# Hybrid diffusion backbone: modulation sums on VectorE in halves, gates kept as rows

## The chip, the cores and the metric

One core of a Trainium2 chip runs the whole program in one launch. The metric is device time in microseconds, the median of three executions; a profile of one more execution gives the trace.

## The reference, cut to what matters

Two layers act on 256 latent tokens and 256 context tokens of width 1024, all in fp32. What the change touches is the adaptive modulation: each layer has one matrix `w_ada` of 1024 x 6144, and two condition vectors are multiplied with it, one for the latent tokens, one for the context.

```python
for layer in range(2):
    need_ctx = layer < 1
    ada_lat = silu(c) @ w_ada[layer] + b_ada[layer]          # 6144 numbers
    ada_ctx = silu(c_ctx) @ w_ada[layer] + b_ada[layer]
    sh1, sc1, g1, sh2, sc2, g2 = split(ada_lat, 6)           # and the same for ada_ctx
    u = modulate(rmsnorm(h, gains[0]), sh1, sc1)             # x * (1 + scale) + shift
    p = u @ w_in[layer]                                      # feeds three parallel mixers
    m = merge(hyena(p), rglru(p), hgrn2(p)) @ w_out[layer]
    h = h + g1 * rmsnorm(m, gains[1])
    f = square(relu(modulate(rmsnorm(h, gains[2]), sh2, sc2) @ w_mlp1[layer])) @ w_mlp2[layer]
    h = h + g2 * rmsnorm(f, gains[3])
```

The second layer needs the context only where the mixers scan through it, so `g1`, `sh2`, `sc2`, `g2` are needed there for the latent tokens alone. The Hyena mixer also needs, once per layer, an implicit filter (a small network with two sines, then a Fourier transform); the kernel calls this `filters(l)`.

## The kernel before

**Products.** Every large matrix is split into a high part (rounded by ScalarE, `wh`) and a low part (the rest, by VectorE, `wl`), and every product is three matmuls. A weight of 1 MB comes by DMA into one of two raw buffers (`ra`), is split at priority 400, and serves 48 matmuls of 512 columns in layer 0. The split parts have four buffers each.

**Modulation.** The 6144 columns of `w_ada` are taken as three thirds of 2048. Third 0 holds shift 1 and scale 1, third 1 holds gate 1 and shift 2, third 2 holds scale 2 and gate 2. In the names below a pair such as (0,1) is layer and third.
- Third (0,0) is needed at once and is made by `ada_first` on TensorE, in quarters.
- Third (0,1) is made by `ada_steps` on TensorE: eight steps, each a load of 1 MB into a raw buffer and four matmuls with a stationary operand of 32 columns, placed on the four column groups of the array, so that they run side by side.
- (0,2), (1,0), (1,1), (1,2) are made by `ada_sums` on VectorE: a *plan* loads four tiles of 128 x 512 (256 KB each) into the four buffers `AM`, and VectorE multiplies each with one column of the condition (`cst`) and adds it to a sum. With both conditions wanted, a plan takes eight such instructions, otherwise four. The sums still lie across 128 partitions; one group of four matmuls with a stationary operand that has ones in one column (`sel`) adds the partitions up.
- `ada_out` copies the four rows out of PSUM, turns all 2048 values into columns by four transposes, adds the bias to them, and, for thirds 1 and 2, also makes gate rows (times the gain, through DRAM, later broadcast by `gate_rows`).

`AM` serves the HGRN2 mixer too, which relies on zeros in it; `ada_sums` ends with four zeroing instructions on GpSimd.

**Order.** The program is written in one order; a scheduler at build time lists it per engine, taking by a model of the durations the ready instruction with the best priority (written order, moved up inside `high_priority`). So work that is ready early can stand ahead of where it is written, if its buffers are free. In passages marked `InOrder.fixed` the listed order is kept as written. Background work comes from the queue `bg`: a list of generators, of which `bg.step()` runs the first one up to its next `yield`, and `bg.drain()` runs all to the end. In layer 0 there is one `bg.step()`:
- for each weight of the input projection that is used (lines 1300 to 1316), and in the merge of the three branches for each weight of the gates and of the branch projections (2 after the first branch's gates, then 4 + 2, then 4 + 2);
- for each of 16 weights of the first MLP product (line 1636), then for each of 8 and 6 weights of the second one (`pump`, line 1648).

`bg.drain()` stands ahead of the output projection (line 1528), and in `start_next` (line 1651), which is called at the layer boundary inside `junction`: the first of four token tiles has its residual, then `norm()` calls `start_next`, then come the norm of tile 0, tile 1 likewise, and a passage in fixed order with transposes, modulation and the first products of layer 1. `groups(filters(1), (9, 4, 4, 9))` cuts the 26 pieces of the second layer's filters into four steps.

```python
        def norm():
            if not holder: holder.append(start_next())   # bg.drain(); lnexp(); Norm(...)
...
        for i in range(2):
            products(i, 0)
            products(i, 1)
            residual(first[i], p[i], G, i)
            n = norm()
            n.tile(i)
```

**Tables.** `era(name)` loads an activation table and orders all later activations that need a table (`fn`) behind it, and itself behind all earlier ones. `filters` asks for the set with Sin; `lnexp()` for that with Ln and Exp, which each residual and each norm uses.

`tmp()` takes one of 14 buffers of 128 x 512, `blk()` one of 49; a PSUM bank comes from `psm()` (`pm`, large products) or `psx()` (`px`, the rest).

Of the kernel before, what the change touches and what calls it, by code (L numbers as in the profile page):

```python
# [96 lines left out]
def prepare(inp):  # L97
# [11 lines left out]
    for w in range(2):  # L109
        for n in range(2):  # L110
            c = (w + 1) * 2048 + (2 * w + n) * 512
            for l in range(2):
                for r in range(2):
                    o = 32 * (2 * n + r) + w if (l, w) == (0, 1) else 32 * (2 * w + n) + r
                    rows[l, w, o] = g["norm_gains"][l, 1 + 2 * w, n * 512:n * 512 + 512]
                    bias[l, w, o] = g["b_ada"][l, c:c + 512]
# [46 lines left out]
def _body(ctx, tc, I, out, cfg):  # L163
# [153 lines left out]
    AM = []  # L317
# [8 lines left out]
    sel = kt([128, 2, 32])  # L326
    pool.memset(sel, 0.0)
    for r in range(2):
        pool.memset(sel[:, r, r:r + 1], 1.0)
# [42 lines left out]
    def ada_steps(l, s):  # L372
        acc = psx('a')
        for k in range(8):
            raw = raw_tile()
            dma(raw, I["w_ada"][l, k * 128:k * 128 + 128, s * 2048:s * 2048 + 2048])
            with tc.high_priority(cfg["AP"]):
                for j in range(4):
                    mm(acc[32 * j:32 * j + 32, :], cst[:, k, :], raw[:, j * 512:j * 512 + 512], k == 0, k == 7,
                       tile_position=(0, 32 * j))  # L380
            yield
        ada_out(l, s, acc, "(j r)")
        yield

    def ada_out(l, s, acc, order):
# [3 lines left out]
        pt = psx('a')  # L389
        for b in range(4):  # L390
            pe.transpose(pt[:, b * 128:b * 128 + 128], rows[:, b * 128:b * 128 + 128], ident)
        cols = kt([128, 2, 2, 8], name="ac")
        if order == "(j r)":
            pv = pt.rearrange("p (b m n r) -> p r m n b", b=4, m=2, n=2)
        else:
            pv = pt.rearrange("p (b n r m) -> p r m n b", b=4, n=2, r=2)[:, :, :2]
        for r in range(2):
            for m in range(2):
                add(cols[:, r, m].rearrange("p (n b) -> p n b", b=4), pv[:, r, m],
                    col(l, "ba", 16 * s + 8 * m, 8).rearrange("p (n b) -> p n b", b=4))  # L400
        ada_cols[l, s] = cols
        if s > 0:
            w, j0 = s - 1, 2 * (s - 1)
# [6 lines left out]
            for n in range(2):  # L410
                if order == "(j r)":
                    dma(st[:, n, :], gr[32 * (j0 + n):32 * (j0 + n) + 2, :])
                    continue
# [1420 lines left out]
```

## Time and profile before

| | |
|---|---|
| median of 3 runs | 1487.9 us (1484.55 to 1488.62) |
| the profiled execution | 1488.52 us, of which the span of the trace is 1486.7 us |
| busy: TensorE, VectorE, ScalarE, GpSimd | 1456.6, 1072.7, 745.4, 25.2 us |
| VectorE sums of `ada_sums` | 168 multiply-adds (117.3 us) and 24 multiplications (10.3 us) |
| matmuls of `ada_steps` | 64 records of two passes each over 32 matmuls (8.3 us) |
| mean granted TensorE clock | 0.995 of full speed |

Times in the trace are microseconds from the span's start. Busy matmuls include waiting inside the array's pipeline, so the start of the next matmul tells more than a matmul's own duration. In a group of instructions, `px<-t,k` names what is written (PSUM tile `px`) and what is read (the moving operand `t`, the stationary operand `k`); buffer numbers are left out. All helpers stand in one line of the source (L220), so the tiles' names tell the work apart: `k` stands for any tile that is kept, `AM` and `cst` among them.

### The profile page before, as it was taken

How to read it: one execution, taken by the hardware profiler on the slowest of the kernel's cores; microseconds unless marked ns; L12 is line 12 of the kernel's file. 1: busy time of each engine (PE TensorE's matmuls, PEld its weight loads, DVE VectorE, ACT ScalarE, POOL GpSimd, SP SyncE). 2: the span in 40 equal slices, each digit the busy share in tenths (PEclk: the TensorE clock that was granted, in tenths of full speed). 3: DMA queues.
4: the chain of work that ended last, by engine and by line, in shares of the span. 5: the costliest groups of instructions: out<-in, count | busy, mean ns of one | idle time of the engine just before them, and what ended most of it. 6: DMA issues, size and time to landing. Idle time of an engine off the chain costs nothing.

```text
span 1486.7 us, 21716 instructions
## 1 busy us (share of the span) xinstructions
PE 1456.6 (98%) x8326; PEld 1224.5 (82%) x8326; DVE 1072.7 (72%) x1853; ACT 745.4 (50%) x1188; POOL 25.2 (2%) x245
## 2 busy tenths in 40 slices
PE   8999999999999999999999999999999999999998
PEld 4766878888888888888887877798889999899986
DVE  6776397978996277755757985776799886866544
ACT  6476565642232425543331223568877745565433
POOL 1000000000000000000000000000000000000000
PEclk9999999999999999999999999999999999999999
DMA  9644321232562242545745534132325335445553
GB/s 316 233 182 160 127 86 58 73 112 86 177 242 91 99 140 88 176 157 189 269 147 208 201 130 141 58 143 85 114 88 178 147 138 204 156 171 186 198 196 113
DMA packets 56999, 225.38 MB, mean 152 GB/s; under 512 B 6448, under 2 KB 8112, under 8 KB 37312
## 3 DMA queue, kind: packets, MB, share of 16 engines
q1 hardware_dynamic: 55168, 220.86, 42.3%
q10 hardware_dynamic: 1728, 3.15, 0.6%
q8 instruction: 65, 1.06, 0.3%
q14 instruction: 38, 0.31, 0.1%
HBM read 220.80 MB, written 3.18 MB: 151 GB/s over the span
## 4 chain that ended last, share of the span: by engine, by line
PE 82%; DVE 9%; ACT 5%; issue 2%; DMA 1%; SPq 0%; DVEq 0%; POOL 0%; ACTq 0%; POOLq 0%
PE pm L220 73%; PE px L220 9%; DVE b L220 4%; DVE t L220 2%; DVE wl L220 2%; ACT b L220 2%; ACT t L220 2%; ACT wh L220 1%; DVE s L220 1%; ACT L220 1%; DMA h<-in_x_dram 1%; DMA k<-in_w_ada_dram 0%; DMA ra<-in_w_ada_dram 0%; DVE h L220 0%; ACT s L220 0%
## 5 line engine op out<-in xcount | busy, mean ns | idle before, releaser
L220 PE MATMUL pm<-b,wh 128*128 128x512 f32 (+1 forms) x3264 | 822.0, 342 | 1.7 <-DVE b L220 1.7
L220 PEld LDWEIGHTS pm<-b,wh 128*128 128x128 f32 x3264 | 564.0, 190 | 76.2 <-issue 3.5
L220 PE MATMUL pm<-b,wl 128*128 128x512 f32 (+1 forms) x1632 | 556.8, 341 | 0.0
L220 ACT ACTIVATE wh<-ra 128x1024 fp32r<-128x1024 f32 x278 | 293.5, 1060 | 498.2 <-PE pm L220 485.3
L220 DVE TENSOR_TENSOR wl<-ra,wh 128x1024 fp32r<-128x1024 f32 x278 | 338.4, 1222 | 243.1 <-ACT wh L220 235.3
L220 PEld LDWEIGHTS pm<-b,wl 128*128 128x128 f32 x1632 | 310.3, 190 | 34.7 <-issue 1.3
L220 PE MATMUL pm<-wh,b 128*128 128x512 f32 x976 | 304.3, 392 | 1.1 <-DVE b L220 1.1
L220 PEld LDWEIGHTS pm<-wh,b 128*128 128x128 f32 x976 | 182.4, 188 | 46.3 <-issue 3.6
L220 PE MATMUL pm<-wl,b 128*128 128x512 f32 x488 | 190.7, 391 | 0.0
L220 DVE TENSOR_TENSOR b<-b,b 128x512 fp32r<-128x512 f32 (+2 forms) x179 | 120.5, 681 | 30.4 <-PE pm L220 14.7
L220 DVE SCALAR_TENSOR_TENSOR t<-k,k,t 128x512 f32<-128x512 f32 x168 | 117.3, 747 | 15.6 <-DMA k<-in_w_ada_dram 15.6
L220 PEld LDWEIGHTS pm<-wl,b 128*128 128x128 f32 x488 | 91.6, 188 | 20.5 <-issue 1.6
L220 PE MATMUL pm<-b,b 128*128 128x256 f32 (+1 forms) x456 | 77.3, 324 | 2.3 <-DVE b L220 2.3
L220 ACT ACTIVATE t<-t 128x512 f32<-128x512 f32 (+3 forms) x124 | 60.8, 526 | 30.7 <-DVE t L220 29.6
L220 PEld LDWEIGHTS pm<-b,b 128*128 128x128 f32 x456 | 66.7, 190 | 10.1 <-DVE b L220 3.6
L220 ACT ACTIVATE t<-pm 128x512 f32<-128x512 f32 (+1 forms) x74 | 42.4, 574 | 35.8 <-PE pm L220 33.3
L220 ACT ACTIVATE b<-pm 128x512 f32<-128x512 f32 x88 | 50.5, 583 | 18.9 <-PE pm L220 10.9
L220 PE MATMUL px<-b,b 128*128 128x128 f32 (+1 forms) x280 | 55.3, 344 | 2.1 <-ACT b L220 1.3
L220 ACT ACTIVATE b<-b 128x512 f32<-128x512 f32 (+1 forms) x80 | 48.7, 627 | 10.7 <-DVE b L220 9.6
L220 ACT ACTIVATE b<-b,k 128x512 f32<-128x512 f32 x64 | 45.7, 739 | 8.6 <-DVE b L220 8.3
L220 PEld LDWEIGHTS px<-b,b 128*128 128x128 f32 x280 | 38.4, 190 | 12.6 <-issue 6.0
L220 ACT ACTIVATE t<-px 128x384 f32<-128x384 f32 (+3 forms) x50 | 21.9, 438 | 46.8 <-PE px L220 46.6
(114 smaller groups left out, 1060.3 us busy)
## 6 DMA issues: line engine op xcount, KB each, us to landing
ra<-in_w_mlp_dram SPq DMA_DIRECT2D x63, 1024.0 KB, 4.9
ra<-in_w_in_dram SPq DMA_DIRECT2D x58, 1024.0 KB, 4.9
k<-in_w_ada_dram SPq DMA_DIRECT2D x128, 256.0 KB, 3.8
ra<-in_w_proj_dram SPq DMA_DIRECT2D x12, 1024.0 KB, 4.8
b<-in_w_ada_first_dram SPq DMA_DIRECT2D x32, 256.0 KB, 5.3
ra<-in_w_ada_dram SPq DMA_DIRECT2D x8, 1024.0 KB, 5.8
ra<-in_w_out_dram SPq DMA_DIRECT2D x8, 1024.0 KB, 5.2
ra<-in_w_i_dram SPq DMA_DIRECT2D x4, 1024.0 KB, 4.7
```

Of the source, the lines that this page charges most:

```text
L220: r = f(*a, **k)
```

## The change

- `ada_steps` is gone: (0,1) is summed by `ada_sums`.
- A job of `ada_sums` is now (layer, third, half), where a half of 1024 columns with both conditions takes four plans of eight instructions, and a third with one condition (half `None`) eight plans of four. Two lists take the place of the old ones. In the merge of layer 0: (0,1) first and second half, (0,2) first half, without zeroing. After the output projection: (0,2) second half, (1,0) in halves, (1,1), (1,2), with zeroing. So it is 12 plans where there were 8, then 28 where there were 24.
- Each half is reduced and handed to `ada_out` by itself. A half that is a gate gets no transposes and no columns. A third with one condition gets columns for one.
- `modulation(1, 1)` fills in one stream; the layouts of `gate_rows` and `sel` follow.

```diff
--- before.py
+++ after.py
@@ -110,8 +110,8 @@
         for n in range(2):
             c = (w + 1) * 2048 + (2 * w + n) * 512
             for l in range(2):
-                for r in range(2):
-                    o = 32 * (2 * n + r) + w if (l, w) == (0, 1) else 32 * (2 * w + n) + r
+                for r in range(2 - l):
+                    o = 32 * (2 * n + r) if l == 0 else 32 * (2 * w + n)
                     rows[l, w, o] = g["norm_gains"][l, 1 + 2 * w, n * 512:n * 512 + 512]
                     bias[l, w, o] = g["b_ada"][l, c:c + 512]
     a["gate_rows"] = np.stack([rows, bias], axis=3)
@@ -323,10 +323,9 @@
 
     cst = kt([128, 8, 32])
     pool.memset(cst, 0.0)
-    sel = kt([128, 2, 32])
+    sel = kt([128, 32])
     pool.memset(sel, 0.0)
-    for r in range(2):
-        pool.memset(sel[:, r, r:r + 1], 1.0)
+    pool.memset(sel[:, 0:1], 1.0)
     csg = kt([128, 8, 2])
     sigmoid()
     fn(csg, cc, AF.Sigmoid)
@@ -369,38 +368,28 @@
         mul(a0[:, ::-1, ks], part[:, :, 0], col(0, "gain0", 2 * qr, 2)[:, None, :].to_broadcast([128, 2, 2]))
         yield
 
-    def ada_steps(l, s):
-        acc = psx('a')
-        for k in range(8):
-            raw = raw_tile()
-            dma(raw, I["w_ada"][l, k * 128:k * 128 + 128, s * 2048:s * 2048 + 2048])
-            with tc.high_priority(cfg["AP"]):
-                for j in range(4):
-                    mm(acc[32 * j:32 * j + 32, :], cst[:, k, :], raw[:, j * 512:j * 512 + 512], k == 0, k == 7,
-                       tile_position=(0, 32 * j))
-            yield
-        ada_out(l, s, acc, "(j r)")
-        yield
-
-    def ada_out(l, s, acc, order):
+    def ada_out(l, s, acc, half):
 
         rows = tmp()
         dve.tensor_copy(rows, acc)
-        pt = psx('a')
-        for b in range(4):
-            pe.transpose(pt[:, b * 128:b * 128 + 128], rows[:, b * 128:b * 128 + 128], ident)
-        cols = kt([128, 2, 2, 8], name="ac")
-        if order == "(j r)":
-            pv = pt.rearrange("p (b m n r) -> p r m n b", b=4, m=2, n=2)
-        else:
-            pv = pt.rearrange("p (b n r m) -> p r m n b", b=4, n=2, r=2)[:, :, :2]
-        for r in range(2):
-            for m in range(2):
-                add(cols[:, r, m].rearrange("p (n b) -> p n b", b=4), pv[:, r, m],
-                    col(l, "ba", 16 * s + 8 * m, 8).rearrange("p (n b) -> p n b", b=4))
-        ada_cols[l, s] = cols
-        if s > 0:
-            w, j0 = s - 1, 2 * (s - 1)
+        gate = s > 0 and half in (None, s - 1)
+        if half is None or not gate:
+            pt = psx('a')
+            for b in range(4):
+                pe.transpose(pt[:, b * 128:b * 128 + 128], rows[:, b * 128:b * 128 + 128], ident)
+            if (l, s) not in ada_cols:
+                ada_cols[l, s] = kt([128, 2, 2, 8], name="ac")
+            cols = ada_cols[l, s]
+            for m in range(2) if half is None else (half,):
+                for r in range(1 if half is None else 2):
+                    if half is None:
+                        pv = pt.rearrange("p (b m n x) -> p x m n b", b=4, m=2, n=2)[:, 0, m]
+                    else:
+                        pv = pt.rearrange("p (b n r x) -> p x r n b", b=4, n=2, r=2)[:, 0, r]
+                    add(cols[:, r, m].rearrange("p (n b) -> p n b", b=4), pv,
+                        col(l, "ba", 16 * s + 8 * m, 8).rearrange("p (n b) -> p n b", b=4))
+        if gate:
+            w = s - 1
             gr, br = tmp(), tmp()
             dma(gr, I["gate_rows"][l, w, :, 0])
             dma(br, I["gate_rows"][l, w, :, 1])
@@ -408,50 +397,39 @@
             mul(gr, gr, rows)
             st = dr.tile([2, 2, 512], F32, name=nm("gd"))
             for n in range(2):
-                if order == "(j r)":
-                    dma(st[:, n, :], gr[32 * (j0 + n):32 * (j0 + n) + 2, :])
-                    continue
-                for r in range(2):
-                    o = 32 * (2 * n + r) + w
+                for r in range(2 if half is not None else 1):
+                    o = 32 * (2 * w + n) if half is None else 32 * (2 * n + r)
                     dma(st[r:r + 1, n, :], gr[o:o + 1, :])
             G_rows[l, w] = st
 
-    def ada_sums(l, thirds):
-
-
-
-        plans = [(s, both, i) for s, both in thirds for i in range(8)]
-
-        def pieces(s, both, i):
-
-            if not both:
+    def ada_sums(jobs, zero):
+
+
+
+        plans = [(j, i) for j in jobs for i in range(8 if j[2] is None else 4)]
+
+        def pieces(job, i):
+
+            l, s, half = job
+            if half is None:
                 return [(i, s * 2048 + n * 512, n) for n in range(4)]
-            half, kk = divmod(i, 4)
-            return [(2 * kk + a, s * 2048 + half * 1024 + n * 512, n) for a in range(2) for n in range(2)]
+            return [(2 * i + a, s * 2048 + half * 1024 + n * 512, n) for a in range(2) for n in range(2)]
 
         def load(q, plan):
             k, c, _ = pieces(*plan)[q]
-            dma(AM[q], I["w_ada"][l, k * 128:k * 128 + 128, c:c + 512])
-
-        def rows(acc, w, src, start, stop):
-            for j, g in enumerate((3, 0, 1, 2)):
-                after = last_mm[0]
-                with tc.high_priority(cfg["AP"]):
-                    ins = mm(acc[32 * g:32 * g + 32, :], w, src(g), start, stop, tile_position=(0, 32 * g))
-                if j == 0:
-                    tc.add_manual_dep(ins, after.name, no_sync, reason="behind the products of this step")
+            dma(AM[q], I["w_ada"][plan[0][0], k * 128:k * 128 + 128, c:c + 512])
 
         for q in range(4):
             load(q, plans[0])
-        acc, due = None, []
-        for at_, (s, both, i) in enumerate(plans):
+        due = []
+        for at_, (job, i) in enumerate(plans):
             yield
             while due:
                 due.pop(0)()
-            if i == 0 or (both and i == 4):
+            if i == 0:
                 sums = {}
-            for q, (k, _, n) in enumerate(pieces(s, both, i)):
-                for r in range(1 + both):
+            for q, (k, _, n) in enumerate(pieces(job, i)):
+                for r in range(1 if job[2] is None else 2):
                     c = cst[:, k, r:r + 1]
                     if (r, n) in sums:
                         stt(sums[r, n], AM[q], c, sums[r, n])
@@ -461,30 +439,31 @@
                 if at_ + 1 < len(plans):
                     load(q, plans[at_ + 1])
 
-            def reduce(s=s, both=both, i=i, sums=sums):
-                nonlocal acc
-                if i == 3 or not both:
-                    acc = psx('a')
-                if both:
-                    rows(acc, sel[:, i // 4, :], lambda g: sums[g % 2, g // 2], i == 3, i == 7)
-                else:
-                    rows(acc, sel[:, 0, :], lambda g: sums[0, g], True, True)
-                if i == 7:
-                    ada_out(l, s, acc, "(n r m)" if both else "(j r)")
-            if i == 7 or (both and i == 3):
+            def reduce(job=job, sums=sums):
+                acc = psx('a')
+                for j, g in enumerate((3, 0, 1, 2)):
+                    src = sums[0, g] if job[2] is None else sums[g % 2, g // 2]
+                    after = last_mm[0]
+                    with tc.high_priority(cfg["AP"]):
+                        ins = mm(acc[32 * g:32 * g + 32, :], sel, src, True, True, tile_position=(0, 32 * g))
+                    if j == 0:
+                        tc.add_manual_dep(ins, after.name, no_sync, reason="behind the products of this step")
+                ada_out(job[0], job[1], acc, job[2])
+            if at_ + 1 == len(plans) or plans[at_ + 1][0] != job:
                 due.append(reduce)
         yield
         while due:
             due.pop(0)()
-        for a_t in AM:
-            pool.memset(a_t, 0.0)
+        if zero:
+            for a_t in AM:
+                pool.memset(a_t, 0.0)
         yield
 
     def modulation(l, which):
 
         a, b = kt([128, 2, 8], name="ma"), kt([128, 2, 8], name="mb")
         gain = ("gain0", "gain2")[which]
-        for r in range(2):
+        for r in range(1 if (l, which) == (1, 1) else 2):
             sc = ada_cols[l, 0][:, r, 1] if which == 0 else ada_cols[l, 2][:, r, 0]
             sh = ada_cols[l, 0][:, r, 0] if which == 0 else ada_cols[l, 1][:, r, 1]
             stt(a[:, 1 - r], sc, 1.0, col(l, gain, 0, 8), ALU.add, ALU.mult)
@@ -1495,7 +1474,7 @@
                 sigmoid()
                 gone = True
                 if l == 0:
-                    bg.put(ada_sums(0, ((2, True),)))
+                    bg.put(ada_sums(((0, 1, 0), (0, 1, 1), (0, 2, 0)), False))
             for x in gates:
                 fn(x, x, AF.Sigmoid)
             if bi == 2:
@@ -1581,7 +1560,7 @@
 
 
         if full:
-            bg.put(ada_sums(1, ((0, True), (1, False), (2, False))))
+            bg.put(ada_sums(((0, 2, 1), (1, 0, 0), (1, 0, 1), (1, 1, None), (1, 2, None)), True))
             bg.put(groups(filters(1), cfg["FG"]))
         hb, cache = [], {}
 
@@ -1812,7 +1791,6 @@
         xs.append(x)
     for _ in f0:
         pass
-    bg.put(ada_steps(0, 1))
     S1, es = layer(0, S0, xs)
     layer(1, S1, None, es)
 
```

## Rows read from the trace of the kernel before

**Rows 1.** The page: busy time by engine; the chain that ended last, by engine.
```profile
PE 1456.6 (98%) x8326; PEld 1224.5 (82%) x8326; DVE 1072.7 (72%) x1853; ACT 745.4 (50%) x1188; POOL 25.2 (2%) x245
...
PE 82%; DVE 9%; ACT 5%; issue 2%; DMA 1%; SPq 0%; DVEq 0%; POOL 0%; ACTq 0%; POOLq 0%
```

**Rows 2.** Timeline of TensorE, 89 to 130 us: start, length, operation, shape, count, wait.
```profile
89.81 0.39 PE L220 MATMUL pm<-b,wl 128*128 128x512 f32 x1
90.13 1.07 PE L220 MATMUL px<-ra,k 128*32 128x512 f32 x8
91.13 0.73 PE L220 MATMUL pm<-wh,b 128*128 128x512 f32 x2
...
124.11 0.39 PE L220 MATMUL pm<-b,wl 128*128 128x512 f32 x1
...
129.28 1.06 PE L220 MATMUL px<-ra,k 128*32 128x512 f32 x8 [1.38 <-DMA ra<-in_w_ada_dram]
```

**Rows 3.** Timeline of VectorE, 96 to 133 us.
```profile
96.97 2.35 DVE L220 TENSOR_TENSOR wl<-ra,wh 128x1024 fp32r<-128x1024 f32 x2
...
121.31 1.22 DVE L220 TENSOR_TENSOR wl<-ra,wh 128x1024 fp32r<-128x1024 f32 x1
...
123.04 1.22 DVE L220 TENSOR_TENSOR wl<-ra,wh 128x1024 fp32r<-128x1024 f32 x1
...
132.84 1.22 DVE L220 TENSOR_TENSOR wl<-ra,wh 128x1024 fp32r<-128x1024 f32 x1 [6.76 <-ACT wh L220]
```

**Rows 4.** Groups by shape, whole span: count, busy us, mean ns, idle before.
```profile
L220 PE MATMUL px<-ra,k 128*32 128x512 f32 x64 | 8.3, 603 | 1.4 <-DMA ra<-in_w_ada_dram 1.4
...
L220 DVE SCALAR_TENSOR_TENSOR t<-k,k,t 128x512 f32<-128x512 f32 x168 | 117.3, 747 | 15.6 <-DMA k<-in_w_ada_dram 15.6
```

**Rows 5.** Chain that ended last, 877 to 882 us: start, length, engine, tile, count.
```profile
877.37 1.00 PE px L220 x8
...
881.09 0.44 PE px L220 x4
```

**Rows 6.** DMA issues of the page: count, KB each, us from issue to landing.
```profile
k<-in_w_ada_dram SPq DMA_DIRECT2D x128, 256.0 KB, 3.8
...
ra<-in_w_ada_dram SPq DMA_DIRECT2D x8, 1024.0 KB, 5.8
```

**Rows 7.** Windows: stretch, its length, busy PE, PEld, DVE, ACT, POOL, granted clock, DMA.
```profile
375.00:452.00 77.00, 77.00 (x348) 62.97 (x347) 70.05 (x105) 25.89 (x34) 2.11 (x4) 1.00 0.57 195
...
767.00:855.00 88.00, 86.88 (x389) 70.64 (x388) 74.89 (x129) 18.37 (x22) 2.33 (x4) 1.00 0.53 186
```

**Rows 8.** Timeline of VectorE, the last sums of the first batch.
```profile
441.44 1.41 DVE L220 SCALAR_TENSOR_TENSOR t<-k,k,t 128x512 f32<-128x512 f32 x2
```

**Rows 9.** Timeline of SP's queue, first loads of the output projection.
```profile
509.62 33.30 SPq L632 DMA_DIRECT2D ra<-in_w_out_dram  x4
```

**Rows 10.** Chain that ended last, 889 to 938 us.
```profile
889.97 0.57 PE px L220 x2
...
931.39 2.58 PE px L220 x6
...
937.88 0.69 ACT t L220 x2
```

**Rows 11.** Timeline of ScalarE, 899 to 943 us.
```profile
899.24 0.42 ACT L220 ACTIVATE t<-t 64x256 f32<-64x256 f32 x1 [3.73 <-DVE t L220]
...
938.58 1.28 ACT L220 ACT_TABLE_LOAD   x1
...
941.70 1.28 ACT L220 ACT_TABLE_LOAD   x1
```

**Rows 12.** Timeline of VectorE, 904 to 936 us.
```profile
904.55 0.69 DVE L220 TENSOR_TENSOR t<-px,t 128x512 f32<-128x512 f32 x1
...
934.80 1.41 DVE L220 TENSOR_TENSOR t<-t,px 128x512 f32<-128x512 f32 x2 [1.04 <-ACT t L220]
```

**Rows 13.** Timeline of TensorE at the layer boundary.
```profile
951.85 1.86 PE L220 MATMUL px<-k,t 128*128 128x128 f32 x15 [1.66 <-DVE t L220]
```

## The prediction

> **What bounds the kernel now.** Read the page first. TensorE is busy 98% of the span, and the chain that ended last runs through it for 82%, through VectorE for 9%, ScalarE for 5% [rows 1]. So a TensorE microsecond taken out counts, unless VectorE or ScalarE turns out to be just behind at that place; VectorE's 72% over the span hides stretches that are nearly full. The windows show two of these: 70 of 77 us in the merge of layer 0, and 75 of 88 us around the start of the second MLP product [rows 7]. The granted clock is 1.00 in both, so nothing is to be got back there.
>
> The part that leaves TensorE is seen in its timeline [rows 2]: a group of eight matmuls from w_ada starts at 90.13 and the products go on at 91.13. The product before started at 89.81 and should have been followed 0.23 us later (the pitch of the 512-column products around it), so one group costs 1.09 us. Sixteen records per two groups, 64 in all [rows 4], make eight groups, 8.7 us. The seventh, at 129.28, also waited 1.38 us for its load.
>
> **Terms, part by part.**
>
> 1. *Sums of the third (0,1) off TensorE.* Eight groups go, 8.7 us, and the wait of 1.4 us: -10.1. How much of it stays? VectorE works almost without a break from 96.97 until after the split at 123.04, and then idles 6.76 us [rows 3]. In this stretch it makes the low half of a weight from 121.31 to 122.53, and TensorE uses such a half at 124.11 [rows 2, 3]. With six groups gone by then TensorE would be there 6.5 us earlier, while the work that fills VectorE starts only two or three groups (2 to 3 us) earlier, since TensorE's results release it. The bounds of what is given back are 0 (the split is issued ahead of the recurrence) and 6.5 us (VectorE keeps its times). I take 2.5: the split has priority 400 and should move up, but the trace shows it waiting behind recurrence work.
>
> 2. *Reductions and transposes.* A third summed in two halves needed two groups of selecting matmuls and still does; (0,1) is new among them: +2 groups. One group takes 1.00 us on the chain and costs the 1.09 of above, four transposes take 0.44 [rows 5]. Calls with transposes go from five to six, as gate halves make none. 2 x 1.09 + 0.44 = +2.6 us, certain within 0.5.
>
> 3. *Sums on VectorE.* Six halves with two rows and two thirds with one: 8 x 32 = 256 instructions, 192 before. 64 x 747 ns [rows 4] = 48 us more. In the merge the pump gives 14 steps up to the output projection (2, then 4+2, then 4+2). Twelve plans need one step to start, twelve to run and one to reduce: 14, none spare, where the old list needed 10. But sums run as soon as VectorE is free: the last of this batch's 64 ran at 441.44 [rows 8], and the first weight of the output projection is asked for at 509.62 [rows 9]. So 32 more, 24 us, have 68 us. Hidden: 0; if that cover is gone, six of them (4.5 us) stand ahead of the splits of the merged tiles. In the MLP products four plans more run there with one row each. There each tile serves one instruction and is loaded again, and TensorE lost 1.1 us in the window with nine such plans [rows 7]: 4/9 of it, +0.5 (0 to 2).
>
> 4. *Loads.* Eight loads of 1 MB become 32 of 256 KB in SP's queue. They land 3.8 us after issue, the 1 MB ones after 5.8 [rows 6]; a set of four serves 6.0 us of sums with two rows, 3.0 with one, and what this leaves uncovered is in term 3. They also leave the two raw buffers to the weights, part of term 1. The Trainium skill ("DMA: Bandwidth & Descriptors", Bandwidth) asks for batches of at least 1 MiB, which speaks against this edit. By row 3.8 us for a quarter of the bytes agrees that small ones move fewer bytes per us, but the queue isn't the limit here, so by the rule, too, the sum changes only inside term 3's 0 to 2.
>
> 5. *Where filters(1) go.* This is the price that the diff doesn't show. Between the output projection and the next layer's norm the pump gives 16 + 8 + 6 = 30 steps. Before: 24 plans end in step 25, the reduction is step 26, and the four groups of filters take 27 to 30. They fit exactly. After: 28 plans end in step 29, the last reduction takes step 30, and nothing is left for the filters. They are all written out by the drain in `start_next`, behind tile 0's residual and ahead of its norm, and the `lnexp()` that follows makes the norm's Ln and Exp wait for both Sin.
>    Now: tile 0's residual starts at 937.88 [rows 10], the first transposes wait for VectorE until 951.85, 14.0 us later, of which TensorE idles 1.66 [rows 13], so it has 12.3 us of products as cover. After: the filters' six pieces on TensorE (first and last in [rows 10], together 8.8 us) leave the time before 937.88 and become cover: 21.1 us. The chain: first filter matmul to the end of the second Sin, 889.97 to 899.66, is 9.7 us; a table load of 1.28; then what followed the last of today's three loads, 942.98 to 951.85, is 8.9 [rows 10, 11, 13]. 19.9 us, just under the cover, so the wait of 1.7 would go. Against that, VectorE's eight late pieces of the filters (first and last in [rows 12], 8.8 us together), until now hidden behind weight steps, meet the casts and subtractions of the norm. I let half stand in the way: 4.4 - 1.2 (spare cover) - 1.7 = +1.5. Lower bound -1.7. Upper bound with nothing overlapped: 9.7 + 8.8 on VectorE + 7.7 on TensorE + 10.2 = 36.4, less 21.1, is 15.3 of waiting, 13.6 more than now.
>    Today three table loads stand in this chain, 938.58 to 941.70, because tile 0's Ln and Exp fall under the Sin set; 3.12 us from first to last is two loads of 1.28, the activations between them, and 0.07 [rows 11]. After, two stand there. The Trainium skill ("ScalarE: Activation LUTs", What ACT_TABLE_LOAD costs) gives a drain of 1.38 us to every load and advises batching by set, which the new order breaks. No such drain shows between these loads; with it the two would cost 2.8 us more and the sum would be 1487.8.
>
> 6. *Less work elsewhere.* No columns for gates, one stream of `modulation(1, 1)`, no first zeroing of AM: small instructions on VectorE and GpSimd under TensorE's products. 0.
>
> Sum: -10.1 + 2.5 + 2.6 + 0.5 + 1.5 = -3.0 on the profiled 1488.5 us, 1485.5. That execution lies 0.6 above the median of 1487.9, so I forecast 1485.
>
> **Rivals.**
>
> *All of it is kept* (term 1 in full, the wait in the junction gone): -10.1 + 2.6 - 1.7 = -9.2, 1479. For it: TensorE's idle time is small everywhere, and a new order has every chance to put the splits first. Against: the full stretch of VectorE [rows 3].
>
> *VectorE keeps the early saving*: term 1 gives back its 6.5, the rest as forecast: +1.0, 1489. For it [rows 3]; against: VectorE idles 6.76 us right behind.
>
> *The junction makes it slower.* One mechanism: the filters, written at the drain, take their temporary buffers (six at once, of 14, four more being held by the first halves' results) and VectorE before the norm gets them, and the norm's Ln waits for the second Sin. Its price is up to 13.6 in place of 1.5; without this term the sum is -4.5, so at 9 it is +4.5, and the point from which it decides is some 11 us of TensorE waiting at the layer boundary. Between 9 and 13.6, at 11, the sum is +6.5, the time 1494. For it: nothing spare in the count of steps, 19.9 against 21.1 is close, and tile 1's chain hangs behind the same table load. Against: the residual and the norm have priority 800, and the filters' matmuls are cover.
>
> **Chances.** A run of this kernel tells 0.3% (4.5 us) from no change, so faster is below 1483.4 and slower above 1492.4. Forecast (1482 to 1488): 0.45. All kept: 0.22. VectorE keeps it: 0.15. Slower junction: 0.18. Of the forecast's 0.45 some 0.17 lies below 1483.4. So faster 0.39, same 0.43, slower 0.18. The range runs from just under the full saving, 1477, to the middle of the slow case, 1494; the likeliest case's own range is 1481 to 1489.
>
> **What would show it.** Term 1: no w_ada matmul with raw tiles before 150 us, and the stretch up to the start of the merge shorter by 6 to 10 us; if VectorE keeps it, new TensorE waits for VectorE near 115 to 125. Term 3: the merge no longer, with the last (0,2) sum of the first batch near 475. Term 5: the Sin activations behind tile 0's residual, two table loads there, and a TensorE wait at the first transposes of under 3 us; the forecast falls if that wait is over 8. It would also be wrong if the merge's end showed TensorE waiting for the split merged tiles.

## The result

The changed kernel takes 1502.5 us (median of 4 runs, 1499.8 to 1506.0), the kernel before, run beside it, 1488.3: 1.0103 times as long, interval 1.0086 to 1.012. That is 14.3 us slower, where 1485 was forecast with a range up to 1494. The profiled execution of the changed kernel is the shortest of its four (span 1498.0, before 1486.7), so its rows account for 11.3 us. The other three ran at a lower mean granted clock, 0.986 to 0.990 in place of 0.991; 0.001 of 1500 us is 1.5 us, so by that estimate the lower clock accounts for most of the 3 us by which the median exceeds the profiled run.

The page of the changed kernel, against [rows 1, 4, 6]: TensorE has 2.6 us less to do, VectorE 38.8 us more, and the chain that ended last runs through VectorE for 11% in place of 9%. The group of the sums has grown from 168 instructions to 224; the loads from w_ada land sooner than before, and VectorE's idle time behind them has fallen from 15.6 [rows 4] to 11.8 us, so it isn't they.

```profile
PE 1454.0 (97%) x8282; PEld 1226.5 (82%) x8282; DVE 1111.5 (74%) x1910; ACT 741.9 (50%) x1186; POOL 23.1 (2%) x240
...
PE 80%; DVE 11%; ACT 5%; issue 2%; DMA 2%; SPq 0%; DVEq 0%; ACTq 0%; POOL 0%; POOLq 0%
...
L220 DVE SCALAR_TENSOR_TENSOR t<-k,k,t 128x512 f32<-128x512 f32 x224 | 156.4, 748 | 11.9 <-DMA k<-in_w_ada_dram 11.8
...
k<-in_w_ada_dram SPq DMA_DIRECT2D x160, 256.0 KB, 3.0
```

To see where the time went, cut the span at three groups of sixteen transposes on the chain that ended last: one ahead of the merge of layer 0 (A), one in the junction behind it (B), one just behind the layer boundary (C). The chain of the kernel before, then of the changed one; in the second, the group of fifteen is that of tile 0's norm at the boundary:

```profile
369.25 1.81 PE px L220 x16
...
579.54 1.75 PE px L220 x16
...
967.19 1.75 PE px L220 x16
```

```profile
357.64 1.81 PE px L220 x16
...
576.42 1.75 PE px L220 x16
...
961.90 3.38 PE px L220 x15
...
978.74 1.75 PE px L220 x16
```

With tile 0's last residual (R, 937.88 in [rows 10], 929.20 now) this makes four stretches. Up to A: 11.6 us shorter. A to B (the merge): 210.3 and 218.8, 8.5 longer. B to R (the MLP): 358.3 and 352.8; but six pieces of the filters, 8.8 us of TensorE, have left this stretch, so like for like it is 3.2 longer (8.8 is the pieces' own time in [rows 10]). R to C (the boundary): 29.3 and 49.5, of which 8.8 are the pieces that came in: 11.4 longer. -11.6 + 8.5 + 3.2 + 11.4 = 11.5; the rest of the span, from C on, is 0.3 shorter.

**The boundary.** ScalarE and VectorE there: tile 0's h is updated from 931.90, and its norm could begin with two squares of h. They run at 952.92, directly behind the filters' last copy.

```profile
929.20 0.60 ACT L220 ACTIVATE t<-pm 128x512 f32<-128x512 f32 x1 [6.29 <-PE pm L220]
...
942.52 0.42 ACT L220 ACTIVATE t<-t 64x256 f32<-64x256 f32 x1 [4.46 <-DVE t L220]
942.95 1.28 ACT L220 ACT_TABLE_LOAD   x1
948.70 0.60 ACT L220 ACTIVATE t<-px 128x512 f32<-128x512 f32 x1 [4.46 <-PE px L220]
...
952.43 0.60 ACT L220 ACTIVATE t<-px 128x512 f32<-128x512 f32 x1 [3.13 <-PE px L220]
952.92 0.62 ACT L220 ACTIVATE t<-h 128x512 f32<-128x512 f32 x1
```

```profile
931.90 1.41 DVE L220 SCALAR_TENSOR_TENSOR h<-t,s,h 128x512 f32<-128x512 f32 x2
```

ScalarE idles 3.1 to 4.5 us at a time in this stretch, so the squares aren't kept out by work. TensorE's timeline shows what that costs: waits of 0.85, 0.68, 4.07 and 5.20, 10.8 us where it had 1.66 [rows 13]; and then the same fifteen transposes take 3.38, not 1.86.

```profile
947.54 1.12 PE L220 MATMUL px<-t,t 128*128 128x512 f32 x2 [0.85 <-DVE t L220]
949.34 2.84 PE L220 MATMUL px<-t,t 128*128 128x512 f32 x6 [0.68 <-DVE t L220]
956.25 0.45 PE L220 MATMUL px<-k,t 128*128 128x128 f32 x1 [4.07 <-ACT s L220]
961.90 3.38 PE L220 MATMUL px<-k,t 128*128 128x128 f32 x15 [5.20 <-DVE t L220]
```

**The merge.** VectorE's timeline: the first half's last sum is over at 405.4, the second half's first sum comes at 444.54, three microseconds behind the copy of the first half's reduction. In these 39 us VectorE has room; in the window 375 to 452 it works 50.2 us, 70.1 before [rows 7]. The sums come later instead, seven in a row at 459.80, and behind them the additions and multiplications that free TensorE's accumulators.

```profile
404.67 0.75 DVE L220 SCALAR_TENSOR_TENSOR t<-k,k,t 128x512 f32<-128x512 f32 x1
...
441.48 0.69 DVE L220 COPY t<-px 128x512 f32<-128x512 f32 x1
...
444.54 0.49 DVE L220 TENSOR_SCALAR t<-k,k 128x512 f32<-128x512 f32 x1
...
459.80 4.72 DVE L220 SCALAR_TENSOR_TENSOR t<-k,k,t 128x512 f32<-128x512 f32 x7
...
465.57 1.28 DVE L220 TENSOR_TENSOR b<-pm,b 128x512 f32<-128x512 f32 x2
```

```profile
438.43 1.07 PE L220 MATMUL px<-t,k 128*32 128x512 f32 x8
...
454.74 0.73 PE L220 MATMUL pm<-b,wh 128*128 128x512 f32 x2 [1.41 <-DVE b L220]
466.40 0.91 PE L220 MATMUL pm<-b,wh 128*128 128x512 f32 x2 [3.21 <-DVE b L220]
```

**The MLP.** Between B and R TensorE waits three times for VectorE's halves of the hidden units, 1.63, 0.32 and 0.90 us, where it waited once, 1.12, before. These 1.7 us more and one group and one set of transposes that are new there (1.5 by term 2's prices) are the 3.2.

```profile
769.97 1.19 PE L220 MATMUL pm<-wh,b 128*128 128x512 f32 x4 [1.63 <-DVE b L220]
```

The windows show the merge and the boundary at once: in 452 to 498 TensorE is busy 41.4 of 46 us at a granted clock of 0.96 (46.0 at 1.00 in the kernel before, first line), in 955 to 995 33.6 of 40 at 0.87.

```profile
452.00:498.00 46.00, 46.00 (x207) 37.06 (x207) 24.59 (x33) 13.10 (x17) 0.00 (x0) 1.00 0.30 103
```

```profile
375.00:452.00 77.00, 77.00 (x344) 62.86 (x343) 50.21 (x73) 24.04 (x31) 0.00 (x0) 1.00 0.45 152
452.00:498.00 46.00, 41.38 (x179) 32.52 (x178) 38.78 (x60) 11.85 (x16) 0.00 (x0) 0.96 0.57 188
...
955.00:995.00 40.00, 33.55 (x250) 32.55 (x251) 33.25 (x121) 27.07 (x63) 1.97 (x22) 0.87 0.17 63
```

### The profile page after: what moved, and what is told of

It is laid out like the page before. It is cut to its first block, busy times and chain, and to the rows that moved or that the text cites. A ratio compares the mean times of both kernels' runs of the same rounds, so it can differ in the third digit from the quotient of the medians.

```text
span 1498.0 us, 21738 instructions
## 1 busy us (share of the span) xinstructions
PE 1454.0 (97%) x8282; PEld 1226.5 (82%) x8282; DVE 1111.5 (74%) x1910; ACT 741.9 (50%) x1186; POOL 23.1 (2%) x240
## 4 chain that ended last, share of the span: by engine, by line
PE 80%; DVE 11%; ACT 5%; issue 2%; DMA 2%; SPq 0%; DVEq 0%; ACTq 0%; POOL 0%; POOLq 0%
PE pm L220 70%; PE px L220 9%; DVE b L220 4%; DVE t L220 4%; DVE wl L220 2%; ACT b L220 2%; ACT wh L220 1%; ACT t L220 1%; DMA k<-in_w_ada_dram 1%; DVE s L220 1%; ACT L220 1%; DMA h<-in_x_dram 0%; DVE h L220 0%; ACT s L220 0%; SPq L305 0%
## 5 line engine op out<-in xcount | busy, mean ns | idle before, releaser
L220 DVE SCALAR_TENSOR_TENSOR t<-k,k,t 128x512 f32<-128x512 f32 x224 | 156.4, 748 | 11.9 <-DMA k<-in_w_ada_dram 11.8
L220 PEld LDWEIGHTS pm<-b,b 128*128 128x128 f32 x456 | 66.6, 190 | 10.8 <-DVE b L220 3.6
L220 ACT ACTIVATE b<-b 128x512 f32<-128x512 f32 (+1 forms) x80 | 48.6, 627 | 10.7 <-DVE b L220 9.6
```

The costliest lines, as they stand in the source:

```text
L220: r = f(*a, **k)
```

## The experiments

The kernel before, run beside these kernels, took 1488.3 to 1488.7 us; the ratios are to those runs. Stretches are those of above, in us, read from each profile at the same landmarks. The filters' 8.8 us stand in B to R in the rows marked *, in R to C in the others. Up to A the versions of the changed kernel do the same work, and their profiles still reach A anywhere from 357.6 to 361.7 (the latest two, e10 and e13, have a granted clock of 0.97 in 120 to 200 and 0.98 in 200 to 280, where the changed kernel has 1.00): landmarks of two profiles compare by stretches, not by absolute times.

| kernel | median us | ratio to before, interval | A-B | B-R | R-C |
|---|---|---|---|---|---|
| before * | 1488.3 | | 210.3 | 358.3 | 29.3 |
| after | 1502.5 | 1.0103, 1.0086 to 1.012 | 218.8 | 352.8 | 49.5 |
| e4_third_left_out * | 1477.9 | 0.9933, 0.9914 to 0.9952 | 210.3 | 357.8 | 29.3 |
| e2_filters_in_drain | 1502.8 | 1.0095, 1.0071 to 1.0118 | 210.3 | 347.6 | 54.1 |
| e1_more_steps * | 1487.7 | 1.0006, 0.9987 to 1.0024 | 217.2 | 358.6 | 29.3 |
| e3_free_reduction | 1498.5 | 1.0067, 1.0041 to 1.0093 | 212.2 | 356.0 | 50.5 |
| e8_steps_and_merge_free * | 1479.7 | 0.9948, 0.9931 to 0.9965 | 212.5 | 358.6 | 29.3 |
| e6_other_buffers | 1504.3 | 1.0114, 1.0095 to 1.0134 | 218.8 | 354.7 | 50.0 |
| e7_no_sin_table | 1507.2 | 1.0138, 1.0114 to 1.0162 | 218.8 | 356.9 | 50.8 |
| e9_buffers_and_table | 1504.4 | 1.0112, 1.009 to 1.0135 | 217.1 | 359.3 | 49.5 |
| e10_no_shared_buffers | 1493.1 | 1.004, 1.0024 to 1.0056 | 217.1 | 356.2 | 39.8 |
| e11_no_shared_no_table | 1496.4 | 1.0054, 1.0038 to 1.0071 | 219.8 | 358.1 | 38.7 |
| e12_rows_elsewhere | 1504.4 | 1.011, 1.009 to 1.013 | 212.7 | 357.6 | 50.2 |
| e13_steps_and_rows * | 1489.4 | 1.0005, 0.9993 to 1.0018 | 212.5 | 364.4 | 29.3 |

### What the removed work is worth

e4_third_left_out: the kernel before without the third (0,1); (0,2) stands in for it, so the values differ.

```diff
-    bg.put(ada_steps(0, 1))
```

> The kernel before, with the third (0,1) not computed at all: its columns and gate rows are taken from those of (0,2), so the output is not the reference's. It shows what TensorE and the raw buffers get back by themselves. Forecast's term 1: -7.6, 1480.7 us. All of it kept: -10.1, 1478. What the landmarks of the changed kernel's trace suggest: -11.6, 1476.7. VectorE keeps the saving: 1484.7.

10.3 us less (7.1 to 12.8 by the interval). That is term 1's full 10.1, and its saving is real; the forecast's 7.6 lies inside the interval, near its end, so the times alone don't rule out that some is given back.

### Where the filters stand

e2_filters_in_drain: the kernel before, its filters put in the list only at the layer boundary. e1_more_steps: the changed kernel with four more steps of the pump in the first MLP product.

```diff
-            bg.put(groups(filters(1), cfg["FG"]))
...
             def start_next():
+                bg.put(groups(filters(1), cfg["FG"]))
                 bg.drain()
```

```diff
-            bg.step()
+            bg.step(2 if full and r in (2, 6, 10, 14) else 1)
```

> The kernel before, with the second layer's filters written by the drain at the layer boundary and not in pump steps 27 to 30; nothing else is changed. Theory (the drain is what costs): 1488.3 + 10 to 11.5, 1498 to 1500 us, with TensorE waiting some 10 us at the boundary. Rival (it costs only together with the longer list of sums): within 3 us of 1488.

> The changed kernel, in which four of the sixteen pump steps of the first MLP product run two pieces of background work, so that 34 steps are there for the 28 plans, the reduction and the filters, and the filters run behind weight steps again. Theory (the filters in the drain hold up the layer boundary: 9.9 us there and 1.5 us at a lower clock): 1502.5 - 11 = 1491 us, first transposes of the boundary about 12 us after the residual of tile 0. Rival (the sums themselves crowd VectorE, and the filters only change their place): no more than 3 us gained, 1499 or above.

e2 alone is 14.6 us slower than the kernel before: the move by itself, with no sums or reductions changed, costs as much as the whole change. Its TensorE shows the same two waits, and one more that the changed kernel has not, for the filters' own load, which may be why it is slower than expected. Without these 3.3 us its price is some 11.

```profile
934.53 0.61 PE L220 MATMUL px<-t 17*64 17x256 f32 x2 [3.26 <-DMA t<-in_ff_dram]
...
958.67 0.30 PE L220 MATMUL px<-k,t 128*128 128x128 f32 x1 [4.07 <-ACT s L220]
964.32 3.46 PE L220 MATMUL px<-k,t 128*128 128x128 f32 x15 [5.35 <-DVE t L220]
```

B to R is 10.7 shorter in e2 than before, 1.9 more than the filters' 8.8, of which 1.1 is the MLP's one wait, which is gone. By that measure the changed kernel has lost 5.2 in the MLP and 9.5 at the boundary, not 3.2 and 11.4; their sum stays as it was.

e1 takes 14.8 us off the changed kernel, more than the 11 expected. The boundary is back at 29.3 with one wait, as before the change, and B to R, which has the filters again, at 358.6, so that 2.9 of the 3.2 us that the MLP had lost are gone too: the sums come earlier there (their last reduction runs at 873.61, at 921.97 in the changed kernel), and TensorE waits for VectorE nowhere between B and R.

```profile
948.17 1.86 PE L220 MATMUL px<-k,t 128*128 128x128 f32 x15 [1.65 <-DVE t L220]
```

### Why the norm stands behind the filters

The forecast's slower rival gave two reasons: the filters hold too many of the 14 temporary buffers, and the norm's Ln waits for the second Sin and a table load. e6_other_buffers takes nine of the filters' temporaries (w3, fwd, dec, the products with dec; its expectation counts six) from the pool of 49; e7_no_sin_table computes Exp for Sin in the second layer's filters, without their table loads (other values); e9_buffers_and_table does both.

```diff
-        room = tmp if l == 1 else blk
+        room = blk
```

```diff
-        era("trig_and_small")
+        if l == 0:
+            era("trig_and_small")
...
-        fn(h2, x[:, :256], AF.Sin)
+        fn(h2, x[:, :256], AF.Sin if l == 0 else AF.Exp)
```

> The changed kernel, with the filters still in the drain, but their six long-lived temporaries taken from the other pool of 49 buffers. Theory B (the norm of tile 0 waits for buffers of the pool of 14 that the filters hold): its squares move up from 952.9 to before 945 us, the waits of 4.1 and 5.2 us at the boundary shrink, 5 us or more gained, 1497 or less. Theory T (the norm waits for the table of Ln and Exp, which waits for both Sin): nothing gained, 1502.

> The changed kernel, with Exp in place of the two Sin of the second layer's filters and without their table, so that no table load stands between the residual and the norm; the output is not the reference's. Theory T: 5 us or more gained, 1497 or less, squares of tile 0 right behind its update. Theory B: the squares still wait for the last copies of the filters, at most the 1.3 us of a table load gained, 1501.

> The changed kernel with the edits of both other runs (other buffers for the filters, Exp in place of Sin without a table load; the output is not the reference's). If buffers and table together are the cause, the boundary is as in the kernel before: waits of TensorE there under 3 us, 1488 to 1491 us. If it is VectorE's and ScalarE's own work on the filters that stands in front of the norm, 1497 or more.

None gains, and R to C stays at 49.5 to 50.8: neither reason holds so, and by its expectation e9 spoke for the engines' own work. But in e9, with no table and nine temporaries fewer in the pool, tile 0's squares still run directly behind the filters' last copy, 0.50 us after its start, as they do in the changed kernel (0.49), e6 and e7 (0.50 each), wherever the copy lies:

```profile
958.59 0.60 ACT L220 ACTIVATE t<-px 128x512 f32<-128x512 f32 x1 [3.15 <-PE px L220]
959.09 0.62 ACT L220 ACTIVATE t<-h 128x512 f32<-128x512 f32 x1
```

Among what e6 and e9 leave in the small pool are `e, x` of that copy. This gave the next theory: temporaries of a pool are handed out in the order in which the code is written, so a later-written one (the squares' output) waits until every earlier-written one (e, x of the filters, written by the drain ahead of the norm) has been taken, however many are free. e10_no_shared_buffers takes every temporary of these filters from the other pool; e11_no_shared_no_table has Exp for Sin besides (other values).

```diff
-        room = tmp if l == 1 else blk
-        ff = tmp(p=64, w=388)
+        room, own = blk, blk if l == 1 else tmp
+        ff = own(p=64, w=388)
...
-            x = tmp(p=64)
+            x = own(p=64)
...
-            e, x = tmp(), tmp()
+            e, x = own(), own()
```

> The changed kernel with every temporary of the second layer's filters (coordinates, turns, e and x too) taken from the pool of 49 buffers, so that the filters and the norm behind them share none of the 14. Theory O (the 14 temporaries are handed out in the order in which the code is written, so tile 0's squares can be issued only after the filters' last pair e, x has been handed out, wherever the filters stand in time): the squares of tile 0 run right behind its update, within 4 us of 933 on the scale of the changed kernel, ahead of the filters' last copy; what is left is one thing, the table: the norm's Ln still waits for the second Sin and one load (about 944). TensorE's waits between the residual and the first transposes fall from 10.8 us to 2 to 5, and the time to about 1493 to 1498. Rival, work itself (VectorE and TensorE simply have the filters' pieces to do there, and buffers don't matter): squares may move, but the waits stay within 2 us of 10.8 and the time is 1501 to 1506.

> The run before, and Exp in place of Sin in the second layer's filters, without the two table loads (the filters then hold other values). Theory O: with neither buffers nor a table between them, the norm of tile 0 runs right behind its update (Ln by 936) and the filters' pieces are cover: TensorE's waits at the boundary fall to 0 to 3 us, the time to 1489 to 1494, some 10 below the changed kernel; it was 1504 and 1507 with each of the two edits by halves. Work itself: 1500 or more, waits over 8. If the run before gains and this one gains nothing more, the table costs nothing.

The squares of e10 come ahead of both Sin, 4.4 us behind tile 0's residual (23.7 in the changed kernel), and the copy runs 14.7 us later, among tile 1's work:

```profile
934.93 0.60 ACT L220 ACTIVATE t<-pm 128x512 f32<-128x512 f32 x1 [6.33 <-PE pm L220]
...
939.34 0.63 ACT L220 ACTIVATE t<-h 128x512 f32<-128x512 f32 x1 [1.86 <-DVE h L220]
...
940.63 0.40 ACT L220 ACTIVATE b<-b 64x256 f32<-64x256 f32 x1
945.08 0.42 ACT L220 ACTIVATE b<-b 64x256 f32<-64x256 f32 x1 [4.04 <-DVE b L220]
...
954.04 0.58 ACT L220 ACTIVATE b<-px 128x512 f32<-128x512 f32 x1
```

R to C falls from 49.5 to 39.8, where 29.3 + 8.8 = 38.1 is the work alone; TensorE waits 3.0 us there in place of 10.8, its granted clock stays at 1.00 in the window 955 to 995, and the time falls by 9.4 us, into the range expected. e6 against e10 tells number from order: nine temporaries taken out of the pool bring nothing, the rest of them all of it. No view shows a buffer being handed out; the theory rests on what it foretold here and in e12 below. e11 takes a further 1.1 us off R to C and no time: 1496.4 misses the 1489 to 1494 expected. So 9.7 of the boundary's 11.4 us were the order of the pool, the table is worth 1.1 at most, in one profile, and 0.6 remain.

### The merge and the MLP

e3_free_reduction takes away the dependency that pins each reduction behind the products of its step; e8_steps_and_merge_free takes it away for the first list alone (`if j == 0 and zero:`) and has e1's steps.

```diff
-                    if j == 0:
-                        tc.add_manual_dep(ins, after.name, no_sync, reason="behind the products of this step")
```

> The changed kernel without the order that holds each reduction of sums behind the products of its step; results are the same. Theory (in the merge the next half's sums wait for the reduction of the last one, idle from 405 to 444 us, and then come in front of the multiplications that free PSUM): the second half starts near 410, the waits of 1.4 and 3.2 us and the lower clock in the merge go, 6 us gained, 1496. Rival (VectorE is simply too full in the merge): no gain, 1502; if reductions now make TensorE wait for the sums, slower.

> The changed kernel with four more pump steps for the second list (filters behind weight steps again) and with the reductions of the first list, in the merge, free of the order behind the products of their step. If the two causes are separate and add up: 1487.7 - 4 = 1483.7 us, faster than before by 4 to 5. If the merge's stall only moves: 1487.7.

In both, A to B falls to 212.2 and 212.5, 6.3 to 6.6 less than in the changed kernel. e3 gains 4.0 us only, where 6 were expected: with the reductions of the second list free as well, B to R grows by 3.2, and TensorE waits for the halves of the hidden units that VectorE makes:

```profile
769.24 1.22 PE L220 MATMUL pm<-wh,b 128*128 128x512 f32 x4 [3.10 <-DVE b L220]
```

e8 doesn't touch the second list and is 1479.7 us, 8.9 less than the kernel before and 4 less than expected, since e3's gain of 4.0, which the expectation used, has that loss in it. It is what the change can give, and the best version of the study.

e12_rows_elsewhere keeps the pins and takes the temporaries that follow each reduction from the other pool; e13_steps_and_rows adds e1's steps. By the order theory the next half's sums then need not wait for the rows of the one before.

```diff
-        rows = tmp()
+        rows = blk()
...
-            gr, br = tmp(), tmp()
+            gr, br = blk(), blk()
```

> The changed kernel with the three temporaries that follow each reduction (the copied rows and the two gate rows) taken from the pool of 49, the pinning of the reductions kept. Theory O: the sums of the next half no longer wait for the reduction of the one before: in the merge the second half's first sum comes 20 us or more before its 444.5 of now, the sums end well before the multiplications that free PSUM, TensorE's waits of 1.4 and 3.2 us near 455 and 466 go, and the time falls by 3 to 6 us to 1497 to 1500; the boundary keeps its 10.8 us. Rival (the sums are held by the reduction's place in the order of TensorE, not by buffers): first sum still behind the reduction, time 1501 to 1504.

> Both: four more pump steps in the first MLP product (so that the filters come ahead of the boundary) and the rows elsewhere as in the run before. Theory O: the two effects add up, 1487.7 less 3 to 6, some 1482 to 1485, faster than the kernel before, beside 1479.7 of the version whose first list of reductions was left unpinned. Rival as in the run before: 1487 to 1489.

The second half's sums start at 406.33, directly behind the first half's and 33 us ahead of the first half's reduction at 439.42, and the third half's at 433.46; of the two waits in the merge 0.41 us is left:

```profile
405.67 0.75 DVE L220 SCALAR_TENSOR_TENSOR t<-k,k,t 128x512 f32<-128x512 f32 x1
406.33 1.67 DVE L220 TENSOR_SCALAR t<-k,k 128x512 f32<-128x512 f32 x4
...
433.46 1.67 DVE L220 TENSOR_SCALAR t<-k,k 128x512 f32<-128x512 f32 x4
```

A to B is 212.7, so the hold-up in the merge is the shared pool's as well, as the theory of its order foretold. Here order and number change together, since three temporaries leave the pool, and no run tells them apart at this place. Yet the times miss the expectation by 4 to 7 us: in their profiles both lose in the MLP what they gain in the merge (B to R +4.8 over the changed kernel, +5.8 over e1), at a place of which the theory said nothing. TensorE waits longer there, above all for rows that are copied out. The copy still comes 3.0 us behind its reduction, as in the changed kernel (2.8), but the transposes of the rows now stand directly behind the reduction in TensorE's order, where products stood between them before:

```profile
827.71 1.07 PE L220 MATMUL px<-t,k 128*32 128x512 f32 x8
831.44 0.66 PE L220 MATMUL px<-k,b 128*128 128x128 f32 x4 [2.66 <-DVE b L220]
832.53 2.20 PE L220 MATMUL pm<-wh,b 128*128 128x512 f32 x5 [0.43 <-DVE ac L220]
```

e13 has the same waits at 786.76 (2.23) and 878.80 (1.79). Why the listed order changed so is not shown. That the pool's order kept the sums back in the MLP, and that this was worth its price, fits e3, e12 and e13, which all lose there, but no run tests it by itself.

## Why the prediction was wrong

**Term 1** (-10.1, 2.5 of it given back): the size was right, the give-back wrong. The stretch up to A is 11.6 us shorter in the changed kernel's profile, 7.6 to 11.6 among its versions, most of them above 10.5 and the least at the lower clock; e4 gives 10.3 in time. VectorE's full stretch [rows 3] kept next to nothing back: the one new TensorE wait there is 0.41 us, at 127.84. The idle 6.76 us behind that stretch, named as the argument against, were the better evidence.

**Term 2** (+2.6): right, by parts. One new group and one set of transposes fall in A to B (1.5): e8's is 2.2 longer than before's, 0.54 of it a wait. The others fall in B to R (1.5): e8's is 0.3 longer, with the 1.1 us wait of before gone. One set of transposes, 0.4, has left the stretch up to A.

**Term 3**, merge (0, because the sums run as soon as VectorE is free): +6.3, A to B of the changed kernel less that of e8. 1.6 of it is the granted clock, 0.96 in 452 to 498: e1 has the same two waits at 1.00 and takes 217.2. "If that cover is gone" was bounded at 4.5 and placed at the splits of the merged tiles; it was the freeing of accumulators. The step that failed is the reading of [rows 8]. In the old list the first half of (0,2) was reduced too, but into an accumulator that the second half completed: no rows were copied out and no temporary was taken between the halves, and the second half's sums began 33 us ahead of that reduction:

```profile
416.95 1.67 DVE L220 TENSOR_SCALAR t<-k,k 128x512 f32<-128x512 f32 x4
```

```profile
450.04 1.06 PE L220 MATMUL px<-t,k 128*32 128x512 f32 x8
```

So its early last sum said nothing on a list in which each half's rows take a temporary ahead of the next half's sums. MLP (+0.5, 0 to 2): 1.7 of waiting, the 3.2 less term 2's 1.5; with e1's four steps more, none. The four plans more in the MLP are those of (0,2)'s second half, 32 instructions with two rows, and not four plans with one row each.

**Term 4** (0): agrees, loads land 3.0 us after issue, 3.8 before [rows 6].

**Term 5** (+1.5, upper bound 13.6) is the step that decided: +11.4, or 9.5 by e2's measure. The count of steps held: the filters come out of the drain, with two table loads behind the residual as forecast, and giving them steps (e1) or taking them away (e2) moves 14.8 and 14.6 us. The chain of 19.9 us against a cover of 21.1 did not hold. It let the norm follow the second Sin and one load; in fact all of the filters, to their last copy, stand ahead of it. From residual to transposes it is 23.7 us to the first square and 9.0 from there, 32.7, of which 10.8 have no cover. The term called "I let half stand in the way" was a choice between two bounds with no row behind it, and it should have asked what order the buffers force.

**Term 6** (0): no row contradicts it.

**The rival** "The junction makes it slower" had place, price (9 to 13.6) and threshold (some 11 us of TensorE waiting; 10.8 came). The result lies above its 1494 because the merge (8.5 against 2.6) and the MLP (3.2 against 0.5) added 8.6 us over the terms, term 1 gave only 4.0 more than forecast, and the median lies 3 us above the profiled run. Of its two reasons the table is worth 1.1 us at most; buffers are the cause, by the order in which they are handed out and not, as it said, by how many are held.

What stays open: why VectorE makes the halves of the hidden units later in e6, e7, e9, e10 and e11, which change nothing in the MLP but where the filters' buffers lie or which function they use. What it costs is on record: B to R is up to 6.5 us longer there, with 3.6 (e6) to 6.4 us (e9) of TensorE waiting for these halves in place of 2.9, and with a granted clock of 0.91 to 0.96 in 760 to 800, where the changed kernel has 1.00 (by estimate 1.6 to 3.6 us, the missing share of 40).

## What to carry to other kernels

Background work in a list with counted steps has no slack to be taken for granted. Count the steps before and after, and where the list ends, ask what the last job runs into. With this scheduler two jobs that draw temporaries from one pool are ordered by the text of the program, by what e6 and e10 show even with buffers free: a late job written early holds up an urgent one, whatever its priority, and a pool of its own (e10) or an earlier place (e1) undoes it. Freeing such a hold can also cost elsewhere, as in the MLP here, so free it list by list and measure each (e8 against e3 and e13).

## What the runs showed of the hardware

TensorE's clock made the boundary dearer than its waits. In 950 to 956 TensorE works 2.18 us and the granted clock is 0.90; in 956 to 962 it works 0.55 us, at 0.50, the 1.2 GHz level. When the products come again it is 0.62 in the first 4 us and then 1.00, 2.4 GHz:

```profile
950.00:956.00 6.00, 2.18 (x6) 0.63 (x4) 3.74 (x10) 3.18 (x10) 0.00 (x0) 0.90 0.45 173
956.00:962.00 6.00, 0.55 (x2) 0.29 (x3) 4.67 (x15) 3.22 (x11) 0.00 (x0) 0.50 0.00 1
962.00:966.00 4.00, 4.00 (x19) 3.87 (x20) 3.42 (x12) 3.16 (x8) 0.00 (x0) 0.62 0.02 4
966.00:972.00 6.00, 6.00 (x39) 5.41 (x39) 4.97 (x17) 3.08 (x11) 0.39 (x4) 1.00 0.00 0
```

The fifteen transposes there take 3.38 us, 1.86 before [rows 13]: 1.5 us on top of the 10.8 of waiting. The Trainium skill ("TensorE: Matmul & The Clock Gate", HAM oscillation — how this bites in real kernels) tells of a clock that falls to half where the engine waits for its data between groups of matmuls; the trace agrees, with 0.50 in the stretch of the second long wait, right behind the first.
